# Two heads of a pair as one stream through attention, and alternating products in RWKV units

## The chip, the cores and the metric

The kernel runs on one core of a Trainium2 chip. What counts is the device time of one execution in microseconds (us). Four compute engines work beside each other, each in the order of its own program: TensorE (PE in the profile, its weight loads PEld), VectorE (DVE), ScalarE (ACT) and GpSimd (POOL). SyncE (SP) issues the DMA transfers. TensorE writes its results into banks of PSUM; VectorE and ScalarE read them from there.

## The reference

A float32 model over 512 tokens of 1024 features. The first part has two layers of SwiGLU, mixer and SwiGLU; the second part has one layer of mixer and SwiGLU.

- The mixer of the first part joins three branches: six heads of causal attention with low-rank queries and keys (MLA, query and key 96 wide, value 64), a pooling branch, and six heads of causal attention with forget gates (fox, 64 wide): `logit[t,s] = q_t.k_s * scale + (c[t] - c[s])`, softmax over s <= t, times V.
- The mixer of the second part joins a dilated-window attention (three groups of two heads, 64 wide, mixed by their softmax denominators), an RWKV-7 recurrence (six heads, state 64 x 64) and a complex diagonal state-space branch, each gated.

```python
state = state * w_t + sa[..., None] * b_t + v_t[..., None] * k_t   # RWKV: sa = state a_t, y = state r_t
```

## The kernel before

Features lie on the 128 partitions and tokens on the 512 columns. Weight products are GEMMs of three fp32r products (`mm3`, L201 to L203: high and low parts of weights and activations), from banks tagged A; everything else on TensorE is plain fp32, into banks tagged B. There are four banks of either tag.

Inside a mixer the order of all instructions is made while the program is traced. Each piece of work is a stream: a generator that yields the engine and the assumed duration of its next instruction, or takes and gives back a buffer (`acq`, `rel`), or waits for an event. `Sched.run` keeps a clock for each engine and always takes the stream that could start first, by priority among those nearly as early. The counts in `Sched(...)` (A, B, s, sT and so on) are the buffers that streams can take. The order found is the program's order on each engine. GEMM products (`gemm_stream`, priority 50) fill what the other streams leave.

Heads come in pairs on one 128-partition tile, head 0 on partitions 0 to 63 and head 1 on 64 to 127 (fox and the second part's attention; MLA's queries and keys have a tile of 128 rows per head). Each head and block of 128 queries is one stream, `attn_iter`: it takes one of five `s` buffers, computes scores into a B bank (`scores`, L476), adds the mask and takes the maximum on VectorE (L479, L481, L484), the exponential on ScalarE (L486), scales (L493), transposes through a B bank (L499), copies out (`copy`, L441 or L443, into one of three `sT` buffers) and multiplies with V (L507) into 64 partitions of the pair's A bank. The eight streams of a pair are spawned together in `attn_pair_s`. The second part's attention (`iteration` in `attn2`) is built alike; its product with V (L1511) has 128 stationary columns and 64 moving ones.

In the second part's RWKV phase a unit is one pair of heads and one chunk of 128 tokens, twelve units in all, up to four at a time. Each computes five score blocks per head (L1181 to L1183), one head after the other, each with a bank of its own; inverts a triangular matrix by levels (L1224, L1231, L1248); and then the outputs for both heads into one bank, all of head 0's products ahead of head 1's (L1267 to L1274).

Of the kernel before, what the change touches and what calls it, by code (L numbers as in the profile page):

```python
# [12 lines left out]
ALU = mybir.AluOpType  # L13
# [3 lines left out]
P = 128  # L17
T = 512
# [24 lines left out]
class Ev:  # L43
    """Set when it has been signalled n times."""
# [99 lines left out]
class InOrder:  # L144
    """An engine whose instructions stay behind those traced before them."""
# [8 lines left out]
class Kern:  # L154
# [118 lines left out]
    def prep_end_s(self, ev):  # L273
        """prep_end as a stream; self.rb is known from its start."""
# [108 lines left out]
    def load_w(self, name, idx, width, out):  # L383
        """A chunk of weights, loaded and split; its user releases "w"."""
# [70 lines left out]
    def rsqrt_s(self, v, out):  # L455
        """out = 1 / sqrt(v), [128, 512]"""
# [13 lines left out]
    def scores(self, q, k, kw, s, st, bias, scale, diag=None):  # L470
        """s = exp(scale * (q.k + bias) - max), st = max, -scale * max, sum"""
        nc = self.nc
        yield ("acq", "B")
        ps = self.psB()[:, :kw]
        yield ("P", kw * 0.00168)
        nc.tensor.matmul(ps, q, k, start=True, stop=True)  # L476
# [9 lines left out]
        nc.scalar.activation(s, s, AF.Exp, bias=st[1], scale=scale, accum_out=st[2])  # L486

    def pv_s(self, mp, s, f, vt, kw, po):
        """po = V^T (s * f)^T"""
        nc = self.nc  # L490
        nb = kw // P
        yield ("V", 0.135 + kw * 0.0005)
        nc.vector.tensor_scalar(s, s, f, None, ALU.mult)  # L493
        yield ("acq", "B")
        pt = self.psB()[:, :kw]
        yield ("P", 0.11 * nb)
        for j in range(nb):
            b = slice(j * P, (j + 1) * P)
            nc.tensor.transpose(pt[:, b], s[:, b], self.ident)  # L499
        yield ("acq", "sT")  # L500
        sT = self.t(mp, "sT", (P, self.w_s), bufs=self.n_sT)[:, :kw]
        yield from self.copy(sT, pt, kw)
        yield ("rel", "B")
        yield ("P", 0.115 * nb)
        for j in range(nb):
            b = slice(j * P, (j + 1) * P)
            nc.tensor.matmul(po, vt(j), sT[:, b], start=j == 0, stop=j == nb - 1)  # L507
        yield ("rel", "sT")

    def attn_iter(self, mp, q, k, kw, bias, scale, diag, vt, po, done):  # L510
        yield ("acq", "s")
        s = self.t(mp, "s", (P, self.w_s), bufs=self.n_s)[:, :kw]
        st = self.t(mp, "st", (P, 4), bufs=12)
        sl = [st[:, n : n + 1] for n in range(4)]
        yield from self.scores(q, k, kw, s, sl, bias, scale, diag)
        yield V1
        self.nc.vector.reciprocal(sl[3], sl[2])
        yield from self.pv_s(mp, s, sl[3], vt, kw, po)
        yield ("rel", "s")
        yield ("sig", done)  # L520

    def attn_pair_s(self, mp, heads, vt, scale, prio, y, p, ev):
        """heads: two of (q, k, bias, added to the last 128 keys or None); the pair's output, split. A
        bias without the latter ends at the last key."""
        yield ("acq", "A")
        po = self.psA()
        done = Ev(8)
        for i in range(4):
            kw = (i + 1) * P
            for e, (q, k, bias, diag) in enumerate(heads):  # L530
                it = self.attn_iter(
                    mp, q[:, i * P : kw], k[:, :kw], kw, bias[:, T - kw :] if diag is None else bias[:, :kw], scale, diag,
                    lambda j, e=e: vt(e, j), po[e * 64 : e * 64 + 64, i * P : kw], done,
                )
                yield ("spawn", it, prio + (2 * i + e) * 0.01)
# [7 lines left out]
    def to_tok_s(self, src, out):  # L543
        """[128 features, 512 tokens] -> [128 tokens, 4, 128 features]"""
# [10 lines left out]
    def mix1(self, l, after):  # L555
# [4 lines left out]
        self.n_s, self.n_sT, self.w_s, self.p_load = 5, 3, T, 0.5  # L560
        self.LN = self.EXP = "both"
        sch = self.sch = Sched(self.preload, E1, N1, W1, A=4, B=4, s=5, sT=3, cb=2, sq=1, raw=3, w=2)
# [299 lines left out]
    def prep2_tile(self, k):  # L862
        """As prep_tile, for two norms in a row: x * rms * final gain stays as the residual."""
# [54 lines left out]
    def mix2(self, after):  # L918
# [5 lines left out]
        self.n_s, self.n_sT, self.w_s, self.p_load = 5, 3, 256, 1.05  # L924
        self.LN, self.EXP = "ln", "exp"
        sch = self.sch = Sched(self.preload, E2, N2, W2, A=4, B=4, s=5, sT=3, sq=1, zb=4, gt=2, j=2, jx=1, av=2, u=4, q=5, gl=6, raw=3, w=2)
# [110 lines left out]
        def mm_b(lhsT, rhs):  # L1037
            """One product into a B bank, as the stream's next instruction."""
# [6 lines left out]
        def rwkv_prep(p, pool, bufs):  # L1045
# [4 lines left out]
            # decay  # L1050
# [30 lines left out]
            # in-context rate, keys  # L1081
# [75 lines left out]
        def unit(p, c):  # L1157
# [3 lines left out]
            H = self.t(up, "H", (P, 2, 640), bufs=4)  # per head: A | Lak V | L + I | LakT | MrkT | MrbT  # L1161
# [13 lines left out]
            btok, ktok, vtok = TM[:, 0], TM[:, 1], TM[:, 2]  # L1175
            for e in range(2):
                yield ("acq", "B")
                ps = self.psB()
                yield P8
                ar = AR[hb(e), c].rearrange("p a t -> p (a t)")  # L1180
                nc.tensor.matmul(ps[:, 0:128], AR[hb(e), c, 0], Bt[hb(e), tcol], start=True, stop=True)  # L1181
                nc.tensor.matmul(ps[:, 128:384], Kt[hb(e), tcol], ar, start=True, stop=True)  # L1182
                nc.tensor.matmul(ps[:, 384:512], Bt[hb(e), tcol], AR[hb(e), c, 1], start=True, stop=True)  # L1183
                yield V6
                V.tensor_mul(H[:, e, P:640], ps, ms)
                yield ("rel", "B")
            # per head: the diagonal blocks of L + I, twice | their inverses
# [20 lines left out]
            # (I - L)^-1 applied to [A | Lak V]: blocks of 64 are inverted, applied, and joined  # L1208
# [10 lines left out]
            def left(src, li):  # L1219
                """FT = the masked src, transposed"""  # L1220
# [35 lines left out]
            # outputs given the state at the chunk's start  # L1256
# [4 lines left out]
            yield ("P", 0.72 if c == 0 else 0.95)  # L1261
            for e in range(2):
# [3 lines left out]
                if c:  # L1266
                    nc.tensor.matmul(ps[r, 0:P], W, MrbT, start=True, stop=True)  # L1267
                nc.tensor.matmul(ps[r, P : 2 * P], Gv, MrbT, start=True, stop=False)
                nc.tensor.matmul(ps[r, P : 2 * P], vtok[:, r], MrkT, start=False, stop=True)
                if c < 3:  # L1270
                    if c:
                        nc.tensor.matmul(ps[r, 256:320], W, btok[:, r], start=True, stop=True)
                    nc.tensor.matmul(ps[r, 320:384], btok[:, r], Gv, start=True, stop=False)
                    nc.tensor.matmul(ps[r, 320:384], ktok[:, r], vtok[:, r], start=False, stop=True)  # L1274
# [43 lines left out]
        def pair(p):  # L1318
# [4 lines left out]
            # norm over a head's 64 channels  # L1323
# [113 lines left out]
    def attn2(self, ap, sch, late, zt, zev, rbev, xev):  # L1437
# [6 lines left out]
        # tokens t = 16 i + 4 a + c as (c, a, i) for the dilated groups  # L1444
# [12 lines left out]
        st = self.t(ap, "ast", (P, 2, 3, 2, 4))  # slot, group, (max, sum), tile  # L1457
# [26 lines left out]
        def iteration(g, s, i, vt, po, dn):  # L1484
            yield ("acq", "s")
            q, k = zt[13 + 3 * g], zt[14 + 3 * g]
            r = slice(s * 64, s * 64 + 64)
            lo = max(0, i - 1) if g == 0 else i
            kw = (i - lo + 1) * P
            t = self.t(ap, "s", (P, 256), bufs=5)[:, :kw]  # L1490
            m = m0[:, 256 - kw :] if g == 0 else (m1, m2)[g - 1]
            n = (g * 2 + s) * 4 + i
# [680 lines left out]
```

## Time and profile before

| | |
|---|---|
| Median of 3 runs | 2882.68 us (2876.59 to 2884.71) |
| Profiled execution's span | 2882.3 us |
| TensorE busy | 2840.3 us, 99% |
| VectorE busy | 1640.9 us, 57% |
| ScalarE busy | 1036.8 us, 36% |
| GpSimd busy | 452.9 us, 16% |
| Mean granted TensorE clock | 0.992 |

Busy time of TensorE is the union of its instructions' spans, whose ends are modelled: a short gap between two products can hide under the tail of the first. The time from one start to the next shows what a product costs. Times in the rows are microseconds from the start of the span.

### The profile page before, as it was taken

Reading aid. Unit: us, or ns where it says so; the run is one execution under the profiler, and the core shown is the slowest. Engines: PE = TensorE matmul, PEld = TensorE weight load, DVE = VectorE, ACT = ScalarE, POOL = GpSimd, SP = SyncE. Lnnn points to the kernel's source line nnn. Section 1 sums busy time; section 2 is a strip of 40 time slices with the busy share of each in tenths; the row PEclk is TensorE's granted clock in tenths of the full one; section 3 lists DMA queues with packets and bytes.
Section 4 is the critical chain, followed back from the end, with each engine's and each line's share of the span. In section 5 each row is a group of like instructions: output and inputs, shape, how many; then the busy total and the mean of one; then the engine's idle time right before and its main releaser. Section 6 shows DMA issues by size and latency. Waiting matters only on the chain. (4 is left out here: it accounts for less than half of the span.)

```text
span 2882.3 us, 33436 instructions
## 1 busy us (share of the span) xinstructions
PE 2840.3 (99%) x13036; PEld 2260.4 (78%) x13036; DVE 1640.9 (57%) x2577; ACT 1036.8 (36%) x1590; POOL 452.9 (16%) x368
## 2 busy tenths in 40 slices
PE   8999999999999999999999999999999999999998
PEld 6888877688888888887768788875677878788886
DVE  6454566655445554456565745668767655464554
ACT  4222344432223422235353334453334453332223
POOL 2010111010001200012102101124323102210101
PEclk9999999999999999999999999999998999999999
DMA  3223321222222222233122223352130116322222
GB/s 133 96 95 102 107 99 57 70 95 95 95 95 97 101 95 96 95 101 113 61 67 96 103 102 118 114 181 81 66 113 16 41 61 221 106 97 96 92 99 81
DMA packets 92118, 277.45 MB, mean 96 GB/s; under 512 B 11960, under 2 KB 13368, under 8 KB 91960
## 3 DMA queue, kind: packets, MB, share of 16 engines
q1 hardware_dynamic: 91960, 275.32, 28.1%
q8 instruction: 102, 1.67, 0.2%
q14 instruction: 56, 0.46, 0.1%
HBM read 255.87 MB, written 19.40 MB: 96 GB/s over the span
## 5 line engine op out<-in xcount | busy, mean ns | idle before, releaser
L201 PE MATMUL A<-xin,whi 128*128 128x512 f32 x2368 | 940.2, 397 | 6.3 <-ACT whi L192 5.0
L202 PE MATMUL A<-xin,whi 128*128 128x512 f32 x2368 | 931.4, 393 | 2.5 <-DVE xin L255 2.5
L203 PE MATMUL A<-xin,wlo 128*128 128x512 f32 x2368 | 930.1, 393 | 3.6 <-DVE wlo L193 1.9
L192 ACT CAST whi<-wraw 128x1024 fp32r<-128x1024 f32 (+2 forms) x343 | 349.8, 1020 | 1024.3 <-issue 377.8
L193 DVE TENSOR_TENSOR wlo<-wraw,whi 128x1024 fp32r<-128x1024 f32 (+2 forms) x343 | 500.2, 1459 | 85.6 <-ACT whi L192 59.0
L201 PEld LDWEIGHTS A<-xin,whi 128*128 128x128 f32 x2368 | 446.6, 189 | 115.3 <-issue 19.7
L202 PEld LDWEIGHTS A<-xin,whi 128*128 128x128 f32 x2368 | 446.6, 189 | 101.2 <-DVE xin L255 6.3
L203 PEld LDWEIGHTS A<-xin,wlo 128*128 128x128 f32 x2368 | 446.6, 189 | 97.7 <-DVE wlo L193 3.1
L332 POOL TENSOR_TENSOR u<-u,g 128x512 f32<-128x512 f32 x110 | 158.3, 1439 | 1418.4 <-DVE u L330 1135.5
L202 PE MATMUL B<-hl,whi 128*128 128x512 f32 x880 | 343.5, 390 | 1.9 <-DVE hl L217 1.9
L201 PE MATMUL B<-hh,whi 128*128 128x512 f32 x880 | 342.5, 389 | 0.0
L203 PE MATMUL B<-hh,wlo 128*128 128x512 f32 x880 | 342.4, 389 | 0.0
L341 DVE SCALAR_TENSOR_TENSOR x<-B,x 128x512 f32<-128x512 f32 x120 | 83.0, 692 | 307.1 <-PE B L203 307.1
L330 DVE TENSOR_TENSOR u<-A,rb 128x512 f32<-128x512 f32 x110 | 76.0, 691 | 256.2 <-PE A L203 256.2
L202 PEld LDWEIGHTS B<-hl,whi 128*128 128x128 f32 x880 | 165.2, 188 | 39.6 <-DVE hl L217 5.4
L393 ACT CAST whi<-wraw 128x1024 fp32r<-128x1024 f32 (+2 forms) x117 | 119.8, 1024 | 208.8 <-PE A L202 124.2
L201 PEld LDWEIGHTS B<-hh,whi 128*128 128x128 f32 x880 | 165.2, 188 | 34.9
L203 PEld LDWEIGHTS B<-hh,wlo 128*128 128x128 f32 x880 | 165.2, 188 | 34.0
L395 DVE TENSOR_TENSOR wlo<-wraw,whi 128x1024 fp32r<-128x1024 f32 (+2 forms) x117 | 153.7, 1314 | 22.4 <-ACT whi L393 21.5
L326 DVE TENSOR_TENSOR g<-A,rb 128x512 f32<-128x512 f32 x110 | 75.9, 690 | 157.3 <-PE A L203 157.3
L266 POOL TENSOR_TENSOR ssum<-ssum,sq 128x512 f32<-128x512 f32 x54 | 89.2, 1652 | 376.9 <-ACT sq L265 370.2
L216 ACT CAST hh<-u 128x512 fp32r<-128x512 f32 x110 | 68.6, 623 | 161.4 <-POOL u L332 161.4
(464 smaller groups left out, 2936.4 us busy)
## 6 DMA issues: line engine op xcount, KB each, us to landing
wraw<-in_f2gu SPq DMA_DIRECT2D x88, 512.0 KB, 3.2
wraw<-in_f1gu SPq DMA_DIRECT2D x87, 512.0 KB, 3.2
wraw<-in_w_in SPq DMA_DIRECT2D x76, 512.0 KB, 3.3
wraw<-in_f3gu SPq DMA_DIRECT2D x44, 512.0 KB, 3.2
wraw<-in_f1db SPq DMA_DIRECT2D x32, 448.0 KB, 3.1
wraw<-in_f2db SPq DMA_DIRECT2D x32, 448.0 KB, 3.3
wraw<-in_w_out SPq DMA_DIRECT2D x24, 512.0 KB, 3.3
wraw<-in_f1da SPq DMA_DIRECT2D x16, 512.0 KB, 3.2
```

Source lines behind the costliest of these rows:

```text
L192: nc.scalar.copy(hi[:, b], raw[:, b])
L193: nc.vector.tensor_sub(lo[:, b], raw[:, b], hi[:, b])
L201: mm(ps, wh, xh, start=first, stop=False)
L202: mm(ps, wh, xl, start=False, stop=False)
L203: mm(ps, wl, xh, start=False, stop=last)
L266: (nc.vector if k == NK - 1 else nc.gpsimd).tensor_add(self.ssum, self.ssum, sq)
L326: nc.vector.tensor_mul(g, pg, rb)
L330: nc.vector.tensor_mul(u, pu, rb)
L332: nc.gpsimd.tensor_mul(u, u, g)
L341: nc.vector.scalar_tensor_tensor(self.x[o], ps, scale, self.x[o], ALU.mult, ALU.add)
L393: nc.scalar.copy(hi[:, :width], raw[:, :width])
L395: nc.vector.tensor_sub(lo[:, :width], raw[:, :width], hi[:, :width])
```

## The change

Both heads of a pair become one stream, `attn_block`, per block of 128 queries. `scores2` takes two banks and issues both heads' scores next to each other. Each head's softmax and transposes are a stream of their own (`head`), spawned after the block has taken a pair of `sT` buffers. When both have signalled, the products with V follow, for each block of keys head 0 and then head 1. `s` now counts pairs: two in the first part (four buffers instead of five) and three in the second (six instead of five); `sT` is two pairs (four buffers instead of three). `iteration` in `attn2` gets the same form; its products with V stay one head after the other. The planner's assumed durations change with it.

In an RWKV unit the scores of both heads are issued alternately into two banks, which a new count `B2` allows one unit at a time. In the outputs the two heads' products alternate. Comments and docstrings go too.

```diff
-    def scores(self, q, k, kw, s, st, bias, scale, diag=None):
+    def softmax_s(self, ps, kw, s, st, bias, scale, diag, ev):
         nc = self.nc
-        yield ("acq", "B")
-        ps = self.psB()[:, :kw]
-        yield ("P", kw * 0.00168)
-        nc.tensor.matmul(ps, q, k, start=True, stop=True)
...
+    def scores2(self, pair, kw, half):
+        out = []
+        for _ in pair:
+            yield ("acq", "B")
+            out.append(self.psB()[:, :kw])
+        yield ("P", kw * 0.00168 * (1 if half else 2) + (0.2 if half else 0.0))
+        for ps, (q, k) in zip(out, pair):
+            self.nc.tensor.matmul(ps, q, k, start=True, stop=True)
+        return out
+
+    def attn_block(self, mp, pair, kw, biases, scale, diags, vt, po, done, prio):
...
+        yield ("acq", "s")
+        ss = [self.t(mp, "s", (P, self.w_s), bufs=self.n_s)[:, :kw] for _ in range(2)]
...
+        half = pair[0][0].shape[0] == 64
+        pss = yield from self.scores2(pair, kw, half)
+        soft = Ev(2)
+
+        def head(e):
...
+            yield from self.softmax_s(pss[e], kw, s, sl, biases[e], scale, diags[e], ev)
...
+            yield ("acq", "B")
+            pt = self.psB()[:, :kw]
+            yield ("P", 0.11 * nb)
+            for j in range(nb):
+                b = slice(j * P, (j + 1) * P)
+                nc.tensor.transpose(pt[:, b], s[:, b], self.ident)
+            sT[e] = self.t(mp, "sT", (P, self.w_s), bufs=self.n_sT)[:, :kw]
+            yield from self.copy(sT[e], pt, kw)
+            yield ("rel", "B")
+            yield ("sig", soft)
+
+        sT = [None] * 2
+        yield ("acq", "sT")
+        for e in range(2):
+            yield ("spawn", head(e), prio)
+        yield ("wait", soft)
+        yield ("rel", "s")
+        yield ("P", 0.2 + 0.115 * nb * 2)
         for j in range(nb):
             b = slice(j * P, (j + 1) * P)
...
+            for e in range(2):
+                nc.tensor.matmul(po[e], vt(e, j), sT[e][:, b], start=j == 0, stop=j == nb - 1)
         yield ("rel", "sT")
...
-        self.n_s, self.n_sT, self.w_s, self.p_load = 5, 3, T, 0.5
+        self.n_s, self.n_sT, self.w_s, self.p_load = 4, 4, T, 0.5
...
-        sch = self.sch = Sched(self.preload, E1, N1, W1, A=4, B=4, s=5, sT=3, cb=2, sq=1, raw=3, w=2)
+        sch = self.sch = Sched(self.preload, E1, N1, W1, A=4, B=4, s=2, sT=2, cb=2, sq=1, raw=3, w=2)
...
+            pss = []
             for e in range(2):
+                yield ("acq", "B2")
                 yield ("acq", "B")
-                ps = self.psB()
-                yield P8
+                pss.append(self.psB())
+            yield ("P", 1.2)
+            for e in range(2):
+                nc.tensor.matmul(pss[e][:, 0:128], AR[hb(e), c, 0], Bt[hb(e), tcol], start=True, stop=True)
+            for e in range(2):
                 ar = AR[hb(e), c].rearrange("p a t -> p (a t)")
...
+                nc.tensor.matmul(pss[e][:, 128:384], Kt[hb(e), tcol], ar, start=True, stop=True)
+            for e in range(2):
+                nc.tensor.matmul(pss[e][:, 384:512], Bt[hb(e), tcol], AR[hb(e), c, 1], start=True, stop=True)
+            for e in range(2):
                 yield V6
-                V.tensor_mul(H[:, e, P:640], ps, ms)
+                V.tensor_mul(H[:, e, P:640], pss[e], ms)
                 yield ("rel", "B")
...
-            yield ("P", 0.72 if c == 0 else 0.95)
+            yield ("P", 0.6 if c == 0 else 0.8)
...
+            for both in zip(*parts):
+                for e, (a, b, l, m, first, last, used) in enumerate(both):
+                    if used:
+                        nc.tensor.matmul(ps[hb(e), a:b], l, m, start=first, stop=last)
```

## Rows read from the trace of the kernel before

**Rows 1.** The page, part 1: busy us (share of the span), instructions, by engine.

```profile
PE 2840.3 (99%) x13036; PEld 2260.4 (78%) x13036; DVE 1640.9 (57%) x2577; ACT 1036.8 (36%) x1590; POOL 452.9 (16%) x368
```

**Rows 2.** Stretches: us, busy of PE, PEld, DVE, ACT, POOL, clock, DMA.

```profile
365.00:500.00 135.00, 133.61 (x619) 98.21 (x618) 83.82 (x181) 61.68 (x108) 22.00 (x25) 1.00 0.23 78
500.00:564.00 64.00, 63.31 (x362) 42.02 (x362) 45.30 (x188) 34.32 (x95) 0.00 (x0) 1.00 0.20 62
...
1990.00:2083.00 93.00, 89.24 (x387) 60.84 (x385) 70.66 (x168) 31.81 (x86) 38.77 (x26) 0.94 0.20 68
2160.00:2200.00 40.00, 36.77 (x190) 31.12 (x189) 27.70 (x56) 15.38 (x35) 16.00 (x23) 0.79 0.12 42
2200.00:2362.00 162.00, 161.68 (x1118) 131.43 (x1118) 101.55 (x232) 71.86 (x166) 24.29 (x38) 1.00 0.10 34
```

**Rows 3.** Stretches, L507 (products with V) alone: us, busy of PE and PEld.

```profile
365.00:500.00 135.00, 10.28 (x80) 7.38 (x80) 1.00 0.23 78
500.00:564.00 64.00, 19.93 (x160) 14.37 (x160) 1.00 0.20 62
...
sum 693.00, PE 60.41 PEld 43.50; mean PE 10.07 PEld 7.25
```

**Rows 4.** PE in order of time, products with V: start, us, instructions.

```profile
409.29 0.43 PE L507 MATMUL A<-sT,vt 128*64 128x128 f32 x2
...
508.62 0.66 PE L507 MATMUL A<-sT,vt 128*64 128x128 f32 x8
...
530.10 0.38 PE L499 MATMUL B<-c_ident,s 128*128 128x128 f32 x2
530.41 1.09 PE L507 MATMUL A<-sT,vm 128*64 128x128 f32 x8
531.43 0.33 PE L499 MATMUL B<-c_ident,s 128*128 128x128 f32 x1
...
1511.56 1.58 PE L507 MATMUL A<-sT,vm 128*64 128x128 f32 x16
```

**Rows 5.** PE in order of time, scores of half the rows.

```profile
466.73 0.91 PE L476 MATMUL B<-fk,fq 64*128 64x384 f32 x2
467.57 0.33 PE L499 MATMUL B<-c_ident,s 128*128 128x128 f32 x1
...
2065.77 0.71 PE L476 MATMUL B<-ak,aq 64*128 64x128 f32 x8
```

**Rows 6.** PE in order of time, one RWKV unit's outputs.

```profile
2212.90 0.43 PE L1267 MATMUL B<-H 128*64 128x128 f32 x2
...
2213.73 0.32 PE L1267 MATMUL B<-H 128*64 128x128 f32 x1
2213.78 0.22 PE L1273 MATMUL B<-H,TM 128*64 128x64 f32 x1
```

**Rows 7.** Groups by line and shape, fox scores: busy us, mean ns, idle before.

```profile
L476 PE MATMUL B<-fk,fq 64*128 64x512 f32 x24 | 11.2, 641 | 0.0
...
L476 PE MATMUL B<-fk,fq 64*128 64x128 f32 x24 | 3.0, 322 | 0.0
```

**Rows 8.** Stretches, L476 alone, the second part's attention.

```profile
1990.00:2083.00 93.00, 10.76 (x48) 5.80 (x48) 0.94 0.20 68
```

**Rows 9.** PE in order of time, one RWKV head's scores and what follows.

```profile
2290.92 0.49 PE L1181 MATMUL B<-Bt,AR 64*128 64x128 f32 x2
...
2291.99 0.50 PE L203 MATMUL A<-xin,wlo 128*128 128x512 f32 x1
```

**Rows 10.** PE in order of time, first scores and last products of one block.

```profile
523.41 1.12 PE L476 MATMUL B<-x,qh 128*128 128x512 f32 x2
...
532.99 1.09 PE L507 MATMUL A<-sT,vm 128*64 128x128 f32 x10
```

More of the change, by code (lines that the diff above doesn't have):

```diff
@@ L497, in pv_s @@
         for j in range(nb):
             b = slice(j * P, (j + 1) * P)
[L499 to L507, printed above, removed]
-        yield ("rel", "sT")
@@ L510, in attn_iter @@
[L510 to L519, printed above, removed]
+            for e in range(2):
+                nc.tensor.matmul(po[e], vt(e, j), sT[e][:, b], start=j == 0, stop=j == nb - 1)
@@ L526, in attn_pair_s @@
         po = self.psA()
-        done = Ev(8)
+        done = Ev(4)
         for i in range(4):
             kw = (i + 1) * P
[L530 to L535, printed above, removed]
+            bs = [bias[:, T - kw :] if diag is None else bias[:, :kw] for _, _, bias, diag in heads]
+            it = self.attn_block(
+                mp, [(q[:, i * P : kw], k[:, :kw]) for q, k, _, _ in heads], kw, bs, scale, [h[3] for h in heads], vt,
+                [po[e * 64 : e * 64 + 64, i * P : kw] for e in range(2)], done, prio + 0.02 * i,
+            )
+            yield ("spawn", it, prio + 0.02 * i)
         yield ("wait", done)
@@ L1260, in unit @@
             ps = self.psB()
-            yield ("P", 0.72 if c == 0 else 0.95)
+            yield ("P", 0.6 if c == 0 else 0.8)
+            parts = []
             for e in range(2):
@@ L1265, in unit @@
                 MrkT, MrbT = H[:, e, 384:512], H[:, e, 512:640]
[L1266 to L1274, printed above, removed]
+                parts.append([
+                    (0, P, W, MrbT, True, True, c > 0),
+                    (P, 2 * P, Gv, MrbT, True, False, True),
+                    (P, 2 * P, vtok[:, r], MrkT, False, True, True),
+                    (256, 320, W, btok[:, r], True, True, 0 < c < 3),
+                    (320, 384, btok[:, r], Gv, True, False, c < 3),
+                    (320, 384, ktok[:, r], vtok[:, r], False, True, c < 3),
+                ])
+            for both in zip(*parts):
+                for e, (a, b, l, m, first, last, used) in enumerate(both):
+                    if used:
+                        nc.tensor.matmul(ps[hb(e), a:b], l, m, start=first, stop=last)
             y = vp
@@ new lines, in iteration, with head @@
+            r = [slice(s * 64, s * 64 + 64) for s in range(2)]
+            ts = [self.t(ap, "s", (P, 256), bufs=self.n_s)[:, :kw] for _ in range(2)]
+            pair = [(q[x, i * P : i * P + P], k[x, lo * P : (i + 1) * P]) for x in r]
+            pss = yield from self.scores2(pair, kw, True)
+            soft, sT = Ev(2), [None] * 2
+            def head(s):
+                n = (g * 2 + s) * 4 + i
+                sl = (st[:, s, g, 0, i : i + 1], ng[:, n : n + 1], st[:, s, g, 1, i : i + 1])
+                yield from self.softmax_s(pss[s], kw, ts[s], sl, m, 0.125, None, Ev())
+                yield ("acq", "B")
+                pt = self.psB()[:, :kw]
+                yield ("P", 0.11 * nb)
+                for j in range(nb):
+                    b = slice(j * P, (j + 1) * P)
+                    nc.tensor.transpose(pt[:, b], ts[s][:, b], self.ident)
+                sT[s] = self.t(ap, "sT", (P, 256), bufs=self.n_sT)[:, :kw]
+                yield from self.copy(sT[s], pt, kw)
+                yield ("rel", "B")
+                yield ("sig", soft)
@@ new lines, in iteration @@
+            yield ("acq", "sT")
+            for s in range(2):
+                yield ("spawn", head(s), prio)
+            yield ("wait", soft)
+            yield ("rel", "s")
+            v = lambda s, j: vt[:, (lo + j) * P + s * 64 : (lo + j) * P + s * 64 + 64]
+            yield ("P", 0.23 * nb)
+            for s in range(2):
+                for j in range(nb):
+                    b = slice(j * P, (j + 1) * P)
+                    nc.tensor.matmul(
+                        po[:, i * P + s * 64 : i * P + s * 64 + 64], sT[s][:, b], v(s, j), start=j == 0, stop=j == nb - 1
+                    )
@@ L1522, in group @@
             po = self.psA()
-            dn = Ev(8)
+            dn = Ev(4)
             for i in range(4):
-                for s in range(2):
-                    yield ("spawn", iteration(g, s, i, vt, po, dn), 3 + 0.1 * g + 0.01 * i)
+                prio = 3 + 0.1 * g + 0.01 * i
+                yield ("spawn", iteration(g, i, vt, po, dn, prio), prio)
             yield ("wait", dn)
```

48 lines of the change are left out of this document (15 added, 33 removed).

## The prediction

> **What bounds the kernel now.** I read the page's first part, then a table of stretches, then TensorE's instructions in order of time. The page has TensorE (PE) busy for 99% of the span [rows 1]. Busy time hides gaps behind modelled ends, so the table of stretches comes next [rows 2]: the first block's mixers (365 to 564 us, again from 1315), the second block's attention (1990 to 2083) and its RWKV units (2160 to 2362) all keep PE full, while VectorE stands at 62, 71, 76, 69 and 63% down the rows. PE runs its program in order, and the planner that wrote this order put GEMM products into the gaps of the attention, so PE's own time is what these stages cost. Two exceptions are in the same rows: from 500 us on hardly any GEMM is left to fill with (362 instructions, 160 of them the products with V [rows 3]), and between 2160 and 2200 the clock is 0.79, a mix of the two levels 1.2 and 2.4 GHz, behind waits.
>
> So the question is what PE time the change takes out, and whether what is left still hides the other engines.
>
> **What a product on part of the array costs.** An fp32 product is two instructions, each of two passes: 128 columns take 0.107 us at 2.4 GHz, and the rows keep that pace. The eight instructions of one head's product with V over 512 keys go from 530.41 to the next start at 531.43 [rows 4]: 1.02 us, of which 8 x 0.107 = 0.85 is columns. The other 0.17 is entering and leaving the half-array form, and another 0.09 stands ahead of such a run (two transposes of 0.11 from 530.10 would be done at 530.32). A lone run with half the output columns thus costs 0.26 us beyond its columns; with half the contraction rows 0.30, since 466.73 to 467.57 is 0.84 us for 0.64 of columns [rows 5]. A head alone pays this every time.
>
> That two heads do run side by side when they are adjacent is in the trace of before. Eight score instructions of 128 columns, four of each half of the rows, are busy for 0.71 us in all [rows 5], less than the 0.85 of their columns in sequence. Eight instructions of the product with V take 0.66 us with their tail at 508.62 against 1.09 at 530.41 [rows 4]: two heads of 256 keys against one of 512. The unknown is therefore not whether interleaving works, but how much was there already, and who takes the time freed.
>
> The Trainium skill ("TensorE: Matmul & The Clock Gate", Part 3) has matmuls start and end strictly in program order. The trace differs: the second head's first L1267 starts at 2213.73, ahead of an L1273 of the first head at 2213.78 that precedes it in the program [rows 6], so one half of the array already runs a few instructions ahead of the other. By the page's rule the products with V would be serial now, and the gain from them 51 + 70 x 0.26 - 38 = 31 us; the measured rows give less, below, and decide.
>
> **The change, part by part.** Products with V (L507): 480 instructions are busy 60.4 us [rows 3], in 70 runs, of which the first and the last stand in [rows 4]. A run's busy time counts 0.07 too much (1.09 for 1.02) and lacks the 0.09 ahead, so PE pays 60.4 + 70 x 0.02 = 61.8. After: a pair's four blocks have 10 tiles of keys, 20 instructions of 0.107 for both heads together, and four runs: 2.13 + 4 x 0.26 = 3.17, twelve pairs 38.1. Saved 23.7: per layer 10.28 + 0.2 - 2 x 3.17 = 4.2 before 500 us, and 19.93 + 0.5 - 4 x 3.17 = 7.7 after it.
>
> Scores of the forget-gate heads (L476 with 64 rows): four shapes of 24 instructions, the first and last of them in [rows 7], add up to 28.7 us in 22 runs, so 29.1. After: 2.13 us of columns per pair and three or four runs of 0.30, 18.2 to 20.0 for six pairs. Saved 9.1 to 10.9; I take 10, 1.67 a pair: per layer two pairs before 500 us (3.3) and one after (1.7). The MLA heads' scores use all 128 rows and gain nothing.
>
> Second block's attention: its scores are busy 10.76 us in 15 runs [rows 8], 11.1 with the gaps; after, 3.2 of columns and 12 runs of 0.30, 6.8. Saved 4.3. Its products with V keep the whole array and their order.
>
> RWKV scores: one head is a run from 2290.92 to 2291.99 [rows 9], 1.07 + 0.09 = 1.16. Two heads in turn, into two banks, should cost what one does: 12 x 1.16 = 13.9 saved, 4.6 of it in the first four units near the slow-clock stretch. RWKV outputs: the second head starts 0.82 us after the first (2212.90, 2213.73 [rows 6]) and interleaving removes this lag; six units of the middle chunks 4.9, the six shorter ones (chunk 0 and 3) at half of it 2.4, together 7.3.
>
> VectorE, ScalarE and the DMA queues get no instruction more or less. The added waits are three. A product with V waits for both heads' probabilities; behind it on PE stand the next block's transposes or a GEMM product. A pair's scores wait for two of the four banks. And where five heads could be under way, now two pairs can, with two pairs of transposed tiles that are taken before the softmax and held until the product with V.
>
> **What of it reaches the end.** All of it would be 15.0 (before 500 us, both layers) + 18.8 (the tails, both) + 4.3 + 13.9 + 7.3 = 59.3 us: 2882.3 - 59.3 = 2823. Stretch by stretch: before 500 us there is GEMM work to fill with and VectorE is at 62%, so 15.0 counts whole. In the tails (500 to 564, 1450 to 1514) PE would need 64 - 9.4 = 54.6 us, and VectorE's 45.3 would be 83% of that. There the softmax chains begin to show: a block of 512 keys goes from its first scores at 523.41 to its last product, whose run begins at 532.99 [rows 10], 9.6 us, and two may be under way. I count half, 9.4. The second block's attention has VectorE at 76% and waits of its own: half, 2.1. The RWKV units after 2200 keep PE full beside VectorE at 63%, but each is one chain of small steps: 85% of 16.6, 14.1. Of the first four units' 4.6 a third, 1.5, since PE waits there anyway. Sum 42.1: 2840 us. The profiled execution's span lies 0.4 us under the median of the runs, so it stands for both.
>
> **Rivals.** (a) Everything is realised: 2823. For it: PE is at 98 to 100% in three of the five stretches [rows 2], so little of its time is waiting now. Against it: VectorE at 83% in the tails.
>
> (b) The tails keep their length. Sixteen blocks (four of the last forget-gate pair, twelve MLA) take 64 us now, 4 us each; two under way at 8 us each, less than the 9.6 read for the longest, give the same 64. With nothing from the second block's attention either: 2882.3 - 15.0 - 14.1 - 1.5 = 2852. The Trainium skill ("TensorEngine Tiling (Array Packing)", PSUM Bottleneck) says that packing speeds up TensorE but not the reading of its banks; by that rule this rival is the likelier one. VectorE's 71% in the tail bears it out in part: it is not full yet.
>
> (c) Slower: the pairs lock each other out. A block holds two banks from its scores on and needs two for its transposes; a third block that has taken its scores sits on two of four banks while it waits for transposed tiles. If this leaves 1.4 blocks under way on average, a tail lasts 16 x 8 / 1.4 = 91 us, 27 more, twice; with 30.6 saved elsewhere 2882 + 54 - 31 = 2905. It decides from 16 x 8 / 79 = 1.6 blocks under way on. Against it: a block's own scores give their two banks back before its transposes need any.
>
> (d) The interleaved order does not overlap. Then products with V cost 51.2 + 48 x 0.26 = 63.7, 2 us more than now, scores some 4 more for the overlaps that are lost, and RWKV gives back about as much: 2885, no difference. Against it: [rows 4, 5].
>
> **How the numbers follow.** Forecast 2840: 0.46; (a) 0.18; (b) 0.20; (c) 0.10; (d) 0.06. A measurement tells 0.3% (8.6 us) from no change. Faster by more: 0.46 + 0.18 + 0.20 = 0.84; within: 0.06; slower: 0.10. The range takes in the forecast, (a) and (b), and leaves 0.16 out: low end 2816, where (a) has its runs of scores and of products adjacent and saves another 7 us of form changes (24 fewer runs at 0.30); high end 2864, where (b) gets half instead of 85% from the RWKV units (6 less) and nothing from the first four, with 5 us of new waits, my margin.
>
> **What would show it.** Right: the products with V are busy about 40 us instead of 60.4; RWKV scores stand as one run of 12 instructions in about 1.1 us per unit; the stretch before the first tail is some 7 us shorter and the tail 3 to 9 us; the feed-forward parts are as long as before. Wrong: PE gets gaps in the tail behind VectorE's score reading or ScalarE's exponentials (b), waits of PE for banks before scores or transposes (c), or a slow clock where it is at full speed now.

## The result and the profile after

The changed kernel takes 2849.3 us (median of four runs, 2848.3 to 2853.1), the kernel before 2879.7 in the same set (2876.6 to 2884.7). The ratio is 0.9895 with a 95% interval of 0.9880 to 0.9911: faster by 1.05%, some 30 us. A second set gave 2848.9 against 2880.8, 0.9892. The prediction said 2840 in a range of 2816 to 2864: sign and size hold, but 42 us were forecast. One profiled execution of each kernel is compared below; their spans differ by 35.5 us, since that of before is the slowest of its runs, 5 us over their median. Of all runs in this document one, among the five of after under another plan, took 5701.4 us, twice the other four, and it stands in no ratio.

The page of after, part 1, the line that answers to [rows 1]: busy us, share of the span and instructions by engine.

```profile
PE 2794.3 (98%) x13036; PEld 2221.2 (78%) x13036; DVE 1640.0 (58%) x2544; ACT 1045.9 (37%) x1625; POOL 451.4 (16%) x368
```

TensorE (PE) lost 46 us of busy time and its weight loads (PEld) 39; ScalarE (ACT) gained 9, the others changed by less than 2. Where it went is read from three stretches, each from the last product of one feed-forward part to the first of the next: the first mixer of both layers, then the second block (its attention and RWKV). Columns as in [rows 2]. Of the kernel before:

```profile
375.07:691.32 316.25, 314.17 (x1490) 236.08 (x1488) 191.47 (x437) 136.48 (x253) 39.92 (x36) 1.00 0.24 79
1325.01:1644.01 319.00, 315.28 (x1494) 236.27 (x1492) 209.24 (x534) 140.34 (x261) 43.73 (x38) 1.00 0.25 82
1916.75:2595.06 678.31, 663.59 (x3268) 514.24 (x3267) 440.79 (x744) 254.76 (x458) 168.47 (x154) 0.97 0.28 96
```

Of the kernel after:

```profile
375.60:685.22 309.62, 302.23 (x1489) 227.51 (x1488) 189.67 (x423) 139.44 (x267) 39.33 (x36) 1.00 0.25 81
1318.37:1634.01 315.64, 306.38 (x1493) 229.98 (x1492) 207.44 (x520) 143.31 (x275) 43.16 (x38) 0.99 0.26 83
1906.71:2560.54 653.83, 638.90 (x3269) 490.11 (x3267) 442.19 (x739) 258.09 (x465) 169.35 (x154) 0.99 0.30 99
```

Length less busy time is PE's idle time. In the first mixer PE has 11.9 and 8.9 us less to do, but the stretches are only 6.6 and 3.4 shorter: idle time grew from 2.1 to 7.4 and from 3.7 to 9.3. In the second block PE has 24.7 us less to do with the idle time as before (14.7, 14.9), and nearly all of it arrives (24.5). So the first mixer gave 10.0 us where 24.4 were forecast, the second block 24.5 where 17.7 were.

The products themselves became as short as the change means them to be. PE of after in order of time (start, us, engine, line, tiles, instructions): scores of a pair of forget-gate heads, one RWKV unit's scores and what follows, one unit's outputs and what follows.

```profile
465.16 1.13 PE L493 MATMUL B<-fk,fq 64*128 64x512 f32 x4
466.22 0.50 PE L201 MATMUL A<-xin,whi 128*128 128x512 f32 x1
...
2223.42 0.49 PE L1202 MATMUL B<-Bt,AR 64*128 64x128 f32 x4
2223.75 0.60 PE L1205 MATMUL B<-AR,Kt 64*128 64x256 f32 x4
2224.18 0.39 PE L1207 MATMUL B<-AR,Bt 64*128 64x128 f32 x4
2224.50 0.44 PE L1251 MATMUL B<-c_ident,H 128*128 128x128 f32 x2
...
2228.39 0.66 PE L1305 MATMUL B<-H 128*64 128x128 f32 x8
...
2229.55 0.71 PE L1258 MATMUL B<-C,FT 128*128 128x128 f32 x4
```

Two heads' RWKV scores now take 2223.42 to 2224.50, 1.08 us, what one head took in [rows 9]; the outputs end 1.16 us after they begin. Both are one run of instructions in each of the twelve units.

### The profile page after: what moved, and what is told of

Same layout as the page of the kernel before. It is cut to its first block, busy times and chain, and to the rows that moved or that the text cites. A ratio compares the mean times of both kernels' runs of the same rounds, so it can differ in the third digit from the quotient of the medians.

```text
span 2846.8 us, 33464 instructions
## 1 busy us (share of the span) xinstructions
PE 2794.3 (98%) x13036; PEld 2221.2 (78%) x13036; DVE 1640.0 (58%) x2544; ACT 1045.9 (37%) x1625; POOL 451.4 (16%) x368
## 5 line engine op out<-in xcount | busy, mean ns | idle before, releaser
L193 DVE TENSOR_TENSOR wlo<-wraw,whi 128x1024 fp32r<-128x1024 f32 (+2 forms) x343 | 500.8, 1460 | 86.8 <-ACT whi L192 60.4
L395 DVE TENSOR_TENSOR wlo<-wraw,whi 128x1024 fp32r<-128x1024 f32 (+2 forms) x117 | 155.3, 1327 | 25.9 <-ACT whi L393 25.3
```

The source lines that it names most:

```text
L193: nc.vector.tensor_sub(lo[:, b], raw[:, b], hi[:, b])
L395: nc.vector.tensor_sub(lo[:, :width], raw[:, :width], hi[:, :width])
```

## Where PE's new idle time comes from

PE of after in the first layer, among the forget-gate heads (vt) and around the seam to the MLA heads (vm). In brackets: idle time ahead of the row, and what ended it.

```profile
467.71 0.49 PE L521 MATMUL B<-c_ident,s 128*128 128x128 f32 x3
470.31 0.55 PE L521 MATMUL B<-c_ident,s 128*128 128x128 f32 x3 [2.10 <-DVE s L515]
...
507.78 0.43 PE L537 MATMUL A<-sT,vt 128*64 128x128 f32 x2
...
508.81 0.87 PE L537 MATMUL A<-sT,vt 128*64 128x128 f32 x10
...
511.83 0.43 PE L537 MATMUL A<-sT,vt 128*64 128x128 f32 x2
512.66 1.09 PE L537 MATMUL A<-sT,vt 128*64 128x128 f32 x14 [0.39 <-ACT sT L441]
515.43 0.43 PE L521 MATMUL B<-c_ident,s 128*128 128x128 f32 x2 [1.69 <-DVE s L515]
...
519.53 0.90 PE L521 MATMUL B<-c_ident,s 128*128 128x128 f32 x4 [0.94 <-DVE s L515]
```

And VectorE (DVE) in order of time ahead of the wait that ends at 515.43:

```profile
512.64 1.22 DVE L395 TENSOR_TENSOR wlo<-wraw,whi 128x1024 fp32r<-128x1024 f32 x1
513.78 0.22 DVE L513 RECIPROCAL st<-st 128x1 f32<-128x1 f32 x2
514.40 0.69 DVE L452 TENSOR_TENSOR yl<-A,yh 128x512 fp32r<-128x512 f32 x1 [0.41 <-ACT yh L450]
515.01 0.47 DVE L515 TENSOR_SCALAR s<-s,st 128x128 f32<-128x128 f32 x2
```

The transposes (L521) stand in PE's program ahead of other work and wait for the scaled weights (L515). Ahead of 515.43 the scaling of the next pair is queued on VectorE behind a split of weights and behind L452, which itself waits until the previous pair is through. Waits of this kind are the new ones of after; no wait for a bank is among the longer ones, so rival (c) has no trace. From the waits of PE in after, summed by what ended them (us, times, longest):

```profile
PE B L521 <- DVE s L515: 11.7, 10, 2.1
```

11.7 us, over both layers, is about the idle time that the first mixer gained (5.3 + 5.6). Two explanations stood against each other: with two pairs under way there is no third whose weights are ready (depth), or the planner's softmax durations are too short, so that it places the transposes too early (plan).

The traces show a third cause, which was not among them. The longest wait, 2.10 us at 470.31 and again 2.10 in the second layer, comes where the pooling branch works on GpSimd: two scalings and a split of weights on VectorE take some 2.2 us longer there than the same instructions do elsewhere (rows in the last section). It accounts for 4.2 of the 11.7 us; 7.5 are left for depth or plan.

## The experiments

**Each half alone.** In the first the RWKV scores and outputs are those of before, in the second the attention is.

```diff
-            for e in range(2):
-                nc.tensor.matmul(pss[e][:, 0:128], AR[hb(e), c, 0], Bt[hb(e), tcol], ...)
...
+                nc.tensor.matmul(ps[:, 0:128], AR[hb(e), c, 0], Bt[hb(e), tcol], ...)
...
```

> Only the attention half of the change: RWKV's score and output products are one head after the other again, as before. The theory (each half saves what its own products lose on TensorE) takes from the trace of after that the scores and outputs of RWKV lost 14.7 and 7.2 us, and that their overlap with other work costs a tenth of it: 2849.3 + 20 = 2869 us, that is some 10 us under the kernel before, most of it in the first mixer of both layers. The rival (half-clock stretches move by themselves between any two programs of this kernel, and gave 8 or 9 us of the second mixer's gain) expects a time that isn't the sum: 2860 or less, or 2876 or more, with the half-clock stretches of the second mixer as they were before.

> Only the RWKV half of the change: scores and outputs of a unit's two heads alternate, the attention is that of before. If the halves add, this one is 30.3 us under before less what the attention half gives: 2879.7 - 20 = 2860 us (2856 to 2864), nearly all of the gain in the second mixer, and nothing in the first mixer. If the clock gave part of the second mixer's gain by chance, the second mixer shows the shorter products all the same and the time comes out between 2862 and 2872.

Before took 2882.1 us in this set. Attention alone: 2869.6, ratio 0.9958 (0.9945 to 0.9970), 12.5 us. RWKV alone: 2868.6, 0.9961 (0.9948 to 0.9973), 13.5 us. The first met its number. The second is 6 to 8 us short of what was expected of it and lies in the range of the rival named there (2862 to 2872), that the clock gave part of the second mixer's gain; what the runs say of the clock stands further below. The halves add to 26 us against 30 to 32 together, nearly a sum. The prediction had 26.5 us for the attention (15.0 + 9.4 + 2.1) and 15.6 for RWKV (14.1 + 1.5): the attention was mis-sized by half, RWKV by 2 us.

**RWKV outputs alone**, on the kernel before:

> The kernel before with RWKV's output products alone alternating between the two heads (scores and attention as before). The prediction put them at 7.3 us of TensorE time, of which 85% shorten the kernel: 6 us under before, 2875. The two RWKV parts together gave 13.5 us of some 22 us of product time; if the outputs give their 6, the loss is all with the scores, whose masked products on VectorE now both come after the last product of both heads. If the outputs give 3 or less, both lose alike.

2880.2 us, 0.9991 of before (0.9978 to 1.0003): 2.6 us by the ratio, in an interval that holds both 0 and 6. If the parts add, some 11 of 14 us of the scores' product time reach the end, and a third of the outputs' 7. The expectation that the outputs give 6 and the scores alone lose isn't borne out, but with this interval it isn't excluded either.

**Products with V, one head after the other.** After, with the two loops exchanged:

```diff
-        for j in range(nb):
-            b = slice(j * P, (j + 1) * P)
-            for e in range(2):
+        for e in range(2):
+            for j in range(nb):
+                b = slice(j * P, (j + 1) * P)
```

> After, but the products with V are issued head 0's blocks first and then head 1's, so that the two heads' column halves meet only where the program order puts them together. The prediction took 12 us of TensorE time for their alternation (products with V of 61.8 before to 38.1); the trace of after showed 50.2 to 52 us in 60 runs. If the alternation carries it, the products cost near 60 us of TensorE time again and the kernel takes 2849.3 + 5 to 9 = 2854 to 2858 us. If in these tails the wait for the scaled weights and the transposes decides, the kernel stays within 2 us of after.

2855.4 us, 0.9910 (0.9895 to 0.9926): 4 to 5 us over after by the ratios, at the lower end of what the first theory expected; by the intervals alone the two would not be told apart, but every run of this one (2854.7 to 2857.0) lies above every run of after in both its sets (up to 2853.1). One pair's run of 16 instructions over 512 keys, in this kernel:

```profile
513.57 1.92 PE L537 MATMUL A<-sT,vt 128*64 128x128 f32 x16
```

The same run where they alternate, in the kernel with three pairs (below):

```profile
514.04 1.25 PE L537 MATMUL A<-sT,vt 128*64 128x128 f32 x16
```

So alternation does overlap two heads: rival (d) falls. The products with V are busy for 49.7 us in turn, 43.2 alternating, 60.4 before. They did not come near 60 us again, as the expectation had it, and the 50.2 to 52 us that it names for after are not what this row of after gives, 43.2. Some 60% of what the products lost (10.7 of 17.2 us) comes from the heads standing next to each other at all.

**How many pairs are under way.** After with three pairs; with two, but with the buffers of the transposed weights taken as late as in that one; and with one pair.

```diff
 three pairs (4 -> 6 score buffers; query and key tiles 3 -> 2 to make room, not shown)
-        self.n_s, self.n_sT, self.w_s, self.p_load = 4, 4, T, 0.5
+        self.n_s, self.n_sT, self.w_s, self.p_load = 6, 4, T, 0.5
-        ... A=4, B=4, s=2, sT=2, ...
+        ... A=4, B=4, s=3, sT=4, ...
...
 three pairs, and two with late buffers: each head takes its own, ahead of its transposes
-        yield ("acq", "sT")
+            yield ("acq", "sT")
...
 one pair
...
+        self.n_s, self.n_sT, self.w_s, self.p_load = 2, 2, T, 0.5
+        ... A=4, B=4, s=1, sT=1, ...
```

> After, with three pairs of heads under way in the first mixer in place of two (six score buffers, the transposed weights taken by each head just ahead of its transposes; the query and key tiles of the fox part have two buffers in place of three to make room). Theory 1: with two pairs TensorE runs out of transposes whose weights are scaled, which the trace of after shows as waits of the transposes for VectorE's scaling, 21 us in all over both layers; with a third pair these waits halve and the kernel takes 2840 us (2836 to 2844). Theory 2 (the order was planned with softmax times that are too short, so that transposes stand too early in TensorE's program, whatever the depth): within 2 us of after. Against both: a third pair's scores meet the two banks sooner, and the kernel is slower, 2852 or more.

> The changed kernel itself once more, as the common yardstick of this set: 0.9895 of the kernel before, that is 2852 us where the kernel before takes 2882, and within 2 us of that.

> After, still two pairs under way, but each head takes its buffer for the transposed weights just ahead of its transposes and the pair no longer takes both at its start (the part of the three-pair kernel that isn't the third pair). If the third pair is what gave 7 us there, this one is within 2 us of after. If it was the buffers, which a pair held from its scores to its last product with V, this one is 5 to 7 us faster than after.

> After, with one pair of heads under way in the first mixer in place of two (two score buffers, two of transposed weights). With three pairs the first mixer was shorter than with two; if depth is what keeps the products with V from running as the prediction took them, one pair is worse by more than the third pair gave: 2849 + 8 to 20 = 2857 to 2869 us, with TensorE's waits for scaled weights well over the 11.7 us of after. If the plan covers it with the projection's work, it is within 4 us of after.

> Three pairs under way, once more, to set it against after in a second set of runs: the first gave 0.9875 of before, after had 0.9892 and 0.9895. If the 5 us are real, 0.9865 to 0.9885 again, some 2845 us; if they were a draw, 0.989 or more.

Three pairs: 2845.1 us, 0.9875 (0.9861 to 0.9888), just above the 2836 to 2844 that the first theory expected, and again 2842.2, 0.9861 (0.9837 to 0.9884), inside it. After in its second set: 2848.9, 0.9892. Two pairs with late buffers: 2849.6, 0.9894, so it isn't the buffers. One pair: 2920.1, 1.0130 (1.0108 to 1.0152), slower than the kernel before by 36 us and than after by some 70, far beyond the 8 to 20 expected: the weight of depth was underrated. Some of it is clock: with one pair the first mixer is granted 0.95 and 0.96 of full speed, with two 1.00 and 0.99, which by the lengths of these stretches (345.9 and 346.6 us) is an estimated 28 of the 67 us that they are longer than in after. The eight runs with three pairs lie from 2840.9 to 2847.6, the eight of after from 2847.3 to 2853.1: three pairs are the best version seen, 4 to 7 us under after by the medians, though the intervals of the ratios overlap.

Where it acts is in one row of each kernel: first and last start of the MLA heads' products with V in the first layer (instructions, shortest, median and longest ns). Before, after, three pairs and one pair:

```profile
L507 PE MATMUL A<-sT,vm x120: 272/273/324, 519.7 to 563.2; 128*64 128x128 f32 x120
```

```profile
L537 PE MATMUL A<-sT,vm x120: 272/273/324, 516.7 to 559.3; 128*64 128x128 f32 x120
```

```profile
L537 PE MATMUL A<-sT,vm x120: 272/273/324, 516.9 to 554.8; 128*64 128x128 f32 x120
```

```profile
L537 PE MATMUL A<-sT,vm x120: 272/273/476, 533.0 to 596.0; 128*64 128x128 f32 x120
```

The tail takes 43.5 us before, 42.6 after, 37.9 with three pairs and 63.0 with one; the second layer's rows give 43.5, 42.7, 38.0 and 62.4. The tail alone is not a clean measure, since the planner moves output products across its end: PE's program has 33 instructions of GEMMs in it before, 44 after and 36 with three pairs, and PE is busy for 41.4 of the 42.6 us of after. From the same first start to the next feed-forward part the first layer takes 171.6 us before, 168.5 after, 165.4 with three pairs and 188.7 with one, the second 174.6, 171.6, 168.4 and 191.1. So the change took 3 us a layer here, and the third pair takes another 3. PE's waits with one pair, then with three:

```profile
PE B L521 <- DVE s L515: 29.2, 23, 3.3
```

```profile
PE B L522 <- DVE st L513: 7.5, 2, 3.8
...
PE B L522 <- DVE s L515: 1.4, 4, 0.5
```

29.2, 11.7 and 1.4 us with one, two and three pairs. The third pair leaves one longer wait in each layer (3.8 us), listed under a reciprocal (L513) that was queued on VectorE. What held it is the step of the pooling branch ahead of it, which waits for GpSimd; with three pairs, VectorE and then PE:

```profile
473.24 0.75 DVE L831 SCALAR_TENSOR_TENSOR w<-w,c_invc,w 128x512 f32<-128x512 f32 x1 [4.01 <-POOL w L828]
```

```profile
474.53 1.94 PE L522 MATMUL B<-c_ident,s 128*128 128x128 f32 x8 [3.77 <-DVE st L513]
```

With one pair the same step (L830) stands 3.26 us ahead of the wait of 3.35 that ends at 474.44, and the second layer has its like. Without the waits at the pooling branch 22.5, 7.5 and 1.4 us are left with one, two and three pairs, so depth does cover the softmax chain, and the pooling branch costs PE 2 to 4 us a layer in each of them. The kernel before has the same step (L811), which waits up to 3.8 us for GpSimd, and PE does not wait behind it. No run here took the step away or moved it on purpose.

**The plan.** After and before, each with the planned softmax durations set to the measured ones; only the order of instructions can change.

```diff
-        yield ("V", 0.08 + kw * 0.00104)
+        yield ("V", 0.23 + kw * 0.00105)
...
-        yield ("A", 0.28 + kw * 0.00083, 0, self.EXP)
+        yield ("A", 0.48 + kw * 0.00084, 0, self.EXP)
...
```

> After, with the planned durations of the softmax steps set to those that the trace shows (the sum and maximum 0.23 us + 0.00105 a column in place of 0.08 + 0.00104, the negated maximum 0.15, the exponential 0.48 + 0.00084 in place of 0.28 + 0.00083, the scaling 0.215 + 0.00053 in place of 0.135 + 0.0005): nothing is computed differently, only the order of the instructions is planned with other times. Theory 2 (transposes stand too early in TensorE's program, so TensorE waits for VectorE's scaling, 11.7 us in 10 waits after): those waits halve and the kernel takes 5 us less than after. Theory 1 (two pairs are too few, whatever the plan): within 2 us of after. Slower than after by 2 or more would speak against both: then the time comes with any reshuffling of the order.

> The kernel before, nothing of the change, with the same four planned softmax durations set to the measured ones (the fifth, the reciprocal's, is left). It prices what a new order alone does to this kernel. The theory that the change's 30 us come from shorter products expects that the old order was no bad draw: the kernel before stays within 8 us of itself (2872 to 2889). The rival that any new order may give or take as much as the change did expects 10 us or more to either side; the changed kernel took 15 us more with these durations.

After with this plan: 2864.2 us, 0.9947 (0.9934 to 0.9961), 15 us slower than after. Before with it: 2899.1, 1.0052 (1.0032 to 1.0072), 15 us slower than before. Three things follow. The waits did fall as the plan theory said:

```profile
PE B L521 <- DVE s L515: 3.8, 6, 1.1
PE A L537 <- ACT sT L441: 3.7, 8, 1.3
```

yet the first mixer is 2.8 and 0.1 us longer than in after: a sum of waits is no forecast of the time, and the plan theory falls as a cure. By the words of the expectation, time lost with any new order speaks against both theories; depth rests on the runs with one and three pairs. Most of the loss is in the second block, whose attention is planned with the same durations but has none of these waits for transposes; the row of this kernel:

```profile
1909.78:2574.11 664.33, 641.35 (x3269) 489.98 (x3267) 443.51 (x743) 257.47 (x461) 166.96 (x154) 0.98 0.29 98
```

664.3 us with 23.0 idle, against 653.8 and 14.9. Second, an order alone is worth 15 us in this kernel, half of the change's gain (with before, 7 to 10 us between runs with the same mean granted clock, as below), so a single comparison under one plan could have been luck. Third, it was not: under the other plan the change is worth 0.9947 / 1.0052 = 0.9896 of before, under its own 0.9895 and 0.9892.

**The scaling of a pair's second head (e = 1) on ScalarE:**

```diff
-            nc.vector.tensor_scalar(s, s, sl[3], None, ALU.mult)
+            nc.scalar.mul(s, s, sl[3])
```

> After, with the scaling of the second head of each pair on ScalarE in place of VectorE. If TensorE's waits for scaled weights come from VectorE's queue (its program holds a step that waits for something else, or GpSimd slows it), half of the 11.7 us of those waits go and the kernel takes 3 to 6 us less than after. If ScalarE's longer chain (exponential, scaling and copies of one head all there) takes its place, it is within 2 us of after or slower.

2856.3 us, 0.9922 (0.9908 to 0.9935), 7 us slower than after. The waits for scaled weights from VectorE, now of one head alone, are 11.2 us, as long as before the move. But 6.1 of them are two waits of 3.06 and 3.04 us, one a layer, behind the same step of the pooling branch (L834 here), where VectorE itself waits 2.91 us for GpSimd; without these and those of after, 7.5 us became 5.1. So a lighter queue on VectorE releases some of the waits and the kernel is slower all the same. Where the 7 us go no run shows.

## Why the prediction was nearly right, and where it wasn't

**What bounds the kernel**: right. PE's program was the bound and is still; the feed-forward parts kept their length.

**Sizes of the products.** RWKV: summed over the twelve units from first start to the next instruction's, scores took 28.5 us before and 14.1 after (14.4 less where 13.9 were forecast), outputs 19.0 and 11.8 (7.2 where 7.3 were). Forget-gate scores went from 28.5 to 17.8, forecast from 29.1 to between 18.2 and 20.0. The second block's attention scores 9.9 to 6.8, 3.1 where 4.3 were forecast. Products with V are the term that was mis-sized: 60.4 us of busy time became 43.2, 17 less where 24 were forecast. The step was the four runs a pair, 48 in all. The trace has 60, because twelve blocks are split: two instructions of the first head, other work, then the rest (507.78 and 508.81 above, 2 and 10 instructions). By the prediction's own prices a split adds 0.26 us of entering and leaving and 0.21 of columns beside which nothing runs, 5.6 us for the twelve; that takes its 38.1 to 43.7, against 43.2 + 60 x 0.02 = 44.4 measured. An unsplit run of 16 takes 1.03 us, from 544.45 to the next start, which is 8 x 0.107 + 0.17. So the price of a run was right and the number of runs wrong. That the splits come from the two heads' copies being ready apart is not shown. With three pairs there are 54 runs and 41.5 us.

**What reaches the end.** "Before 500 us there is GEMM work to fill with, so 15.0 counts whole" is the step that failed. From the last feed-forward product to the first MLA product with V the first layer went from 144.6 to 141.1 us, 3.5 shorter where 7.5 were counted before 500 us alone; PE's busy time there fell from 143.2 to 135.0, so its idle time rose by 4.7. The gain was taken back by transposes that wait for scaled weights: the cover was thought of as work, of which there is enough, but a pair's chain is serial and after holds two pairs, where before could run heads singly; and 2.1 us of it is the meeting with GpSimd. The second layer went from 144.4 to 144.0 only. It has the same waits, and besides it two stretches of slow clock where the prediction listed such a clock as a sign of being wrong; the kernel before has 1.00 in all of this mixer (columns as in [rows 2]):

```profile
1340.00:1350.00 10.00, 10.00 (x41) 6.94 (x41) 5.33 (x13) 4.15 (x6) 0.00 (x0) 0.83 0.34 92
1410.00:1420.00 10.00, 7.90 (x41) 5.41 (x38) 8.06 (x20) 3.77 (x9) 6.22 (x7) 0.83 0.18 52
```

The missing share of the clock is 3.4 us in the two. The second of them holds the wait of 2.10 us, which ends at 1414.6; the same wait in the first layer has no slow clock behind it. For the tails half was forecast, 4.7 us a layer, and 3 came: 0.9 in the MLA part, and 2 behind it, where output products had been pulled forward into the tail.

**Rival (b)** said that the tails keep their length because two blocks under way set it. Its number came: it forecast 30.6 us and the runs gave 30.3, where the forecast had 42. That is luck, for its parts did not come: it had 15.0 us before 500 us, nothing from the tails and 15.6 from the second block, and the first mixer gave 10.0 in all, 6 of them from the tails on, and the second block 24.5. The MLA part of the tail did keep its length (43.5 to 42.6), but with eleven more GEMM instructions in it. The test it asked for is the third pair, which shortened the tail by 4.7 us, and by 3 to the end of the mixer. Its arithmetic was too simple: at one block under way it would double the tail, and the row with one pair shows 63.0 for 42.6. **Rival (a)** fell with the first mixer. **Rival (c)**, too few blocks under way, is what one pair does: 2920 us, but by waits for scaled weights and a slower clock, not for banks.

**The second block** gave 24.5 us for 17.7 forecast. A part of this is TensorE's clock, which the prediction left out of the sum. A value between 0.50 and 1.00 is a mix of its two levels, 1.2 and 2.4 GHz. Stretches of 10 us of the kernel before (columns as in [rows 2]):

```profile
1940.00:1950.00 10.00, 8.69 (x27) 5.80 (x26) 8.65 (x14) 1.68 (x2) 5.06 (x5) 0.83 0.49 149
1990.00:2000.00 10.00, 7.99 (x37) 6.30 (x36) 8.47 (x10) 3.49 (x4) 6.86 (x5) 1.00 0.00 0
2010.00:2020.00 10.00, 8.84 (x30) 5.70 (x28) 7.86 (x27) 3.51 (x13) 5.02 (x4) 0.67 0.27 97
2160.00:2170.00 10.00, 8.19 (x45) 6.10 (x44) 8.68 (x18) 4.22 (x9) 6.05 (x11) 0.85 0.23 75
2170.00:2180.00 10.00, 10.00 (x38) 8.65 (x38) 3.24 (x7) 4.82 (x8) 1.82 (x5) 0.50 0.11 43
```

In the stretch ahead of the 0.50 PE was busy for 8.19 us of 10 and in that of the 0.67 for 8.84; 7.99 at 1990 stood with the clock at 1.00. And of after, in about the same part of RWKV's first units:

```profile
2160.00:2170.00 10.00, 7.76 (x46) 5.54 (x46) 5.07 (x10) 4.70 (x8) 7.08 (x13) 1.00 0.15 52
2170.00:2180.00 10.00, 8.63 (x43) 7.23 (x43) 8.15 (x16) 4.05 (x10) 3.76 (x4) 0.83 0.08 28
```

The missing share of the clock, summed over all such stretches of the second block with a clock below 0.97, is 17.2 us before and 8.3 after, 11.9 with the attention alone and 10.3 with RWKV alone. Net of it, by this estimate, the block is 15.6 us shorter, less than the 17.7 forecast: RWKV alone has 9.8 of them, the attention alone nothing.

The clock also moves between runs of one kernel, as the mean granted clock of each run shows. The runs of before take 2876.1 to 2877.5 us at 0.996, 2880.0 to 2881.0 at 0.994 and 2889.6 and 2889.7 at 0.991. Those of after take 2847.3 and 2848.4 at 0.996 and 2848.3 to 2851.0 at 0.994. So at the same clock the change is worth 29 to 31 us, and its gain is not the clock's; the profiled execution of before had 0.992 and that of after 0.994, which goes with the 5 us by which its span lies over the median. Compared in the same way, by the means at each clock, RWKV alone is worth 11 to 12 us, the attention alone 14 to 18, and RWKV's outputs 3 to 5. At the same clock RWKV was thus mis-sized by some 4 us of its 15.6. That the change caused the better clock of the second block was not tried by itself.

## What to carry to other kernels

Price a shorter product by its runs in the trace, then ask what the engine will wait for in the time that comes free: here the softmax chain, covered by a third pair under way, and a step that waits for another engine, which three pairs did not cover. When work is grouped into larger units, count the units that still fit under way, and vary that number in both directions before anything else. When an order is planned by a program, run the change under a second plan; if the ratio stays, as here (0.9895 and 0.9896), the gain belongs to the change.

## What the runs showed of the hardware

VectorE was slower beside GpSimd. The wait that ends at 470.31 has this behind it, VectorE of after:

```profile
465.86 1.29 DVE L515 TENSOR_SCALAR s<-s,st 128x384 f32<-128x384 f32 x1
467.08 2.06 DVE L395 TENSOR_TENSOR wlo<-wraw,whi 128x1024 fp32r<-128x1024 f32 x1
...
469.32 0.93 DVE L515 TENSOR_SCALAR s<-s,st 128x384 f32<-128x384 f32 x1
```

and GpSimd at the same time:

```profile
465.90 1.04 POOL L813 TENSOR_TENSOR w<-w 128x511 f32<-128x511 f32 x1
467.02 3.02 POOL L823 TENSOR_TENSOR w<-w 128x512 f32<-128x512 f32 x2
```

Of the 24 scalings of 384 columns in after, these two and their like in the second layer (1.29 and 0.93) are the ones that a GpSimd instruction overlaps; the other 20 take 0.41 to 0.42 us. In the kernel before and with three pairs none is overlapped, and all 48 take 0.40 to 0.42. L395 took 2.06 here and 1.22 at 512.64, where GpSimd was idle. The Trainium skill ("SBUF — State Buffer", section "SBUF: two separate sides") has the two engines share one pair of ports, which VectorE takes in a two-port mode, or for a second input in SBUF while the GpSimd instruction reads SBUF; the one that starts first holds the pair for its whole instruction. The rows agree that VectorE takes longer while GpSimd works; which of them holds the ports they do not settle: the scaling starts 0.04 us ahead of L813 and is the one that is long, and no row shows its mode.
